# Feed-forward of a hybrid decoder step: gate and up by Strassen block products on normalised features, down projection in two parts

## The chip, the cores and the metric

One core of a Trainium2 chip runs the whole step. The metric is the device time of one execution in microseconds (us). Engines: TensorE (PE), VectorE (DVE), ScalarE (ACT), GpSimd (POOL) and SyncE (SP), whose queue issues most DMAs. Each works through its own queue in order and waits for the others on semaphores.

## The reference

Only the end of the layer is touched. With x the input, `mixed` the gated sum of the three branches:

```python
h = x + rms_norm(mixed @ w_out, norm_mix_post)
f = rms_norm(h, norm_ffn_pre)
f = (silu(f @ w_ffn_gate) * (f @ w_ffn_up)) @ w_ffn_down
y = h + rms_norm(f, norm_ffn_post)
```

There are 544 tokens (512 of the prompt, 32 of the samples), 1024 features in 8 blocks of 128, and 2816 hidden features in 22 blocks of 128. Everything is float32.

## The kernel before

Activations lie transposed, features on partitions and tokens along the columns, in two halves A and B of 272 tokens. A float32 product is made of three `float32r` matmuls: a value x is split into a high part (a cast to float32r, on ACT) and a low part (x minus the high part, on DVE), and the product is high·high + high·low + low·high. `wraw` (L197) loads a weight piece of 128x512 (256 KB) on SP's queue into a ring of five buffers, `wload` and `wk` (L202, L211) split it into `wh` and `wl`, rings of five and four. `dense` (L218) runs the three matmuls of each of k blocks into a PSUM bank per half (L228 to L230) and then calls an evacuation function. `mm_tile` hands out five PSUM banks in turn.

The stretch in question starts with the output projection (`wo`, eight blocks, first for half A, then for half B, evacuated by `normed_evac`, which also sums the squares into `ss1`). `residual(half)` (L1320) follows for each half: `col_stats` turns the sums into one factor per token (matmuls with a column of ones, L282; a root by Newton steps on DVE, L245 to L251, tiles `rs_*`; and matmuls that spread the factor over the partitions, tile `sb`, L299), `h` is scaled and `x` is added (L1328, L1329), the features are split into `fh` and `fl` without their norm (L1330, L1331), and the squares of h are summed into `ss2`. A second `col_stats` makes the factor `R2`.

Gate and up (`gate_up`, L1344): the features go into the product unnormalised, and R2 is multiplied in behind it. Gate: `m_z = p * R2`, `m_a = tanh(m_z / 2)`, `m_g = (m_a + 1) * m_z`, then once more by R2 on POOL (L1352). Up: `m_q = m_g * p`, halved and split into `dh` and `dl` (L1358, L1359). The first four blocks of hidden features (`NA`, list `first_`, weights kept split in slots by `wslots`, tiles `wsh` and `wsl`) run for half A and then for half B; the other 18 run for both halves at once. Then come the down projection over all 22 blocks, and `output`, with a third norm.

The order on each engine is set by a scheduler that walks the program with its own costs; pools and rings (their `bufs`) limit how far it can move things.

Of the kernel before, what the change touches and what calls it, by code (L numbers as in the profile page):

```python
# [157 lines left out]
def step(ctx: ExitStack, tc: tile.TileContext, I, O):  # L158
# [7 lines left out]
    NA, FB = 4, 31  # L166
# [1150 lines left out]
    fh, fl = [fslot("fh", F32R) for _ in range(8)], [fslot("fl", F32R) for _ in range(8)]  # L1317
    ss1, ss2, R2 = slot("ss1"), slot("ss2"), slot("R2")

    def residual(half):  # L1320
# [3 lines left out]
        for n in range(8):  # L1324
            x = htile("xr", 4)
# [4 lines left out]
            S.mul(fh[n][:, s:e], t, gain(G_FPRE + n))  # L1330
            V.scalar_tensor_tensor(fl[n][:, s:e], t, gain(G_FPRE + n), f32(fh[n][:, s:e]), op0=ALU.mult, op1=ALU.subtract)  # L1331
            if n == 0:
                S.square(ss2[:, s:e], t)
            else:
                q = htile("r_q", 2)
                S.square(q, t)
                G.tensor_tensor(ss2[:, s:e], ss2[:, s:e], q, op=ALU.add)
        col_stats(at, [ss2], half, D, R2, tag="at2", bufs=1)
# [4 lines left out]

    def gate_up(j, ws, half, up):  # L1344
        def gevac(p, s, e):
            z = htile("m_z", 2)
            V.tensor_tensor(z, p, R2[:, s:e], op=ALU.mult)
            t = htile("m_a")
            S.activation(t, z, AF.Tanh, scale=0.5)
            g_ = htile("m_g", 4)  # L1350
            V.scalar_tensor_tensor(g_, t, 1.0, z, op0=ALU.add, op1=ALU.mult)  # L1351
            G.tensor_tensor(g_, g_, R2[:, s:e], op=ALU.mult)  # L1352
            gz[j, s] = g_

# [73 lines left out]
```

## Time and profile before

| | |
|---|---|
| median of 3 runs | 1243.65 us (1238.79 to 1243.99) |
| the profiled execution | 1244.79 us, its span 1243.0 us |
| PE busy | 1184.3 us, 95% of the span |
| DVE, ACT, POOL busy | 664.0, 450.2, 325.2 us |
| mean granted clock of PE | 0.981 of full speed |
| chain that ended last | PE 85%, DVE 6%, DMA 4% of the span |

The span runs from the first to the last instruction. Busy times count an engine's instructions from start to end; PE's overlap in its pipeline. The feed-forward takes about the last third of the span.

### The profile page before, as it was taken

What the parts mean: (1) busy time and instruction counts of PE and PEld (TensorE: products, weight loads), DVE (VectorE), ACT (ScalarE), POOL (GpSimd) and SP (SyncE); (2) the same over time, 40 slices, a digit from 0 to 9 for tenths busy, and PEclk for the clock granted to TensorE, in tenths of its full rate; (3) what the DMA queues carried; (4) which work ended last, traced back from release to release, by engine and by line L of the source; (5) the groups of instructions that cost most, each with busy time, mean ns of one, the idle gap of its engine ahead of it and who ended that gap; (6) DMA issues with size and microseconds to landing.
All of it is one profiled execution on the core that took longest, in us unless ns stands there. A gap on an engine that the chain in (4) does not pass through costs nothing.

```text
span 1243.0 us, 24871 instructions
## 1 busy us (share of the span) xinstructions
PE 1184.3 (95%) x9495; PEld 1110.8 (89%) x9495; DVE 664.0 (53%) x1516; ACT 450.2 (36%) x1008; POOL 325.2 (26%) x344
## 2 busy tenths in 40 slices
PE   6999999999799899999899999999999999999996
PEld 6999999978687679789678999999999999999996
DVE  7697574655223223235677859387444544523346
ACT  4334434323122123134446645353333333323341
POOL 6332011211553554400344530034111112100002
PEclk9999999999899899999999999999999999999998
DMA  5332342384686777645121125122222222223343
GB/s 205 98 113 89 123 141 98 104 269 138 200 252 179 228 222 235 203 153 164 37 66 37 47 70 187 52 86 72 85 86 86 94 91 88 86 77 94 94 126 108
DMA packets 87591, 154.87 MB, mean 125 GB/s; under 512 B 11120, under 2 KB 31088, under 8 KB 87472
## 3 DMA queue, kind: packets, MB, share of 16 engines
q1 hardware_dynamic: 73072, 116.57, 29.3%
q0 software_dynamic: 6912, 23.08, 6.2%
q10 hardware_dynamic: 7488, 13.63, 3.4%
q8 instruction: 75, 1.23, 0.4%
q14 instruction: 44, 0.36, 0.1%
HBM read 145.07 MB, written 8.17 MB: 123 GB/s over the span
## 4 chain that ended last, share of the span: by engine, by line
PE 85%; DVE 6%; DMA 4%; issue 3%; ACT 1%; POOL 1%; SPq 0%; DVEq 0%; ACTq 0%; POOLq 0%
PE mm L228 23%; PE mm L229 22%; PE mm L230 22%; PE ps_sc L903 2%; PE po L958 1%; PE pvo L1239 1%; PE pv L1199 1%; PE pk L1184 1%; POOL acc L1128 1%; DMA ret_s<-s 1%; PE ps_sc L910 1%; PE ptm L1232 1%; DMA wr<-w_in 1%; DVE wl L208 1%; DVE ul L335 1%
## 5 line engine op out<-in xcount | busy, mean ns | idle before, releaser
L207 ACT CAST wh<-wr 128x512 fp32r<-128x512 f32 (+2 forms) x316 | 190.6, 605 | 365.8 <-PE mm L229 246.8
L208 DVE TENSOR_TENSOR wl<-wr,wh 128x512 fp32r<-128x512 f32 (+1 forms) x289 | 199.7, 692 | 163.0 <-PE mm L230 104.5
L228 PE MATMUL mm<-uh,wh 128*128 128x272 f32 x896 | 264.9, 297 | 7.9 <-ACT wh L207 5.6
L229 PE MATMUL mm<-ul,wh 128*128 128x272 f32 x896 | 264.1, 295 | 1.9 <-DVE ul L335 1.4
L230 PE MATMUL mm<-uh,wl 128*128 128x272 f32 x896 | 263.2, 294 | 0.4 <-DVE wl L208 0.4
L228 PEld LDWEIGHTS mm<-uh,wh 128*128 128x128 f32 x896 | 170.8, 191 | 13.9 <-ACT wh L207 5.5
L229 PEld LDWEIGHTS mm<-ul,wh 128*128 128x128 f32 x896 | 171.1, 191 | 6.1 <-issue 2.9
L229 PE MATMUL mm<-fl,wh 128*128 128x272 f32 x608 | 175.1, 288 | 0.0
L228 PE MATMUL mm<-fh,wh 128*128 128x272 f32 x608 | 175.0, 288 | 0.0
L230 PEld LDWEIGHTS mm<-uh,wl 128*128 128x128 f32 x896 | 171.3, 191 | 4.0 <-issue 2.9
L230 PE MATMUL mm<-fh,wl 128*128 128x272 f32 x608 | 174.6, 287 | 0.0
L230 PEld LDWEIGHTS mm<-fh,wl 128*128 128x128 f32 x608 | 114.6, 189 | 0.0
L228 PEld LDWEIGHTS mm<-fh,wh 128*128 128x128 f32 x608 | 114.3, 188 | 0.0
L229 PEld LDWEIGHTS mm<-fl,wh 128*128 128x128 f32 x608 | 114.3, 188 | 0.0
L228 PE MATMUL mm<-dh,wh 128*128 128x272 f32 x352 | 101.1, 288 | 0.0
L229 PE MATMUL mm<-dl,wh 128*128 128x272 f32 x352 | 101.1, 288 | 0.0
L230 PE MATMUL mm<-dh,wl 128*128 128x272 f32 x352 | 100.4, 288 | 0.0
L1352 POOL TENSOR_TENSOR m_g<-m_g,R 128x272 f32<-128x272 f32 x44 | 46.1, 1048 | 205.6 <-DVE m_g L1351 194.3
L895 POOL DMA_INDIRECT kt<-kpool,ixk x64 | 61.7, 963 | 85.4 <-DMA kt<-kpool 37.5
L228 PEld LDWEIGHTS mm<-dh,wh 128*128 128x128 f32 x352 | 66.2, 188 | 0.0
L229 PEld LDWEIGHTS mm<-dl,wh 128*128 128x128 f32 x352 | 66.1, 188 | 0.0
L230 PEld LDWEIGHTS mm<-dh,wl 128*128 128x128 f32 x352 | 65.8, 188 | 0.0
(565 smaller groups left out, 2493.8 us busy)
## 6 DMA issues: line engine op xcount, KB each, us to landing
wr<-w_in SPq DMA_DIRECT2D x80, 256.0 KB
wr<-w_fd SPq DMA_DIRECT2D x50, 256.0 KB
wr<-w_fg SPq DMA_DIRECT2D x44, 256.0 KB
wr<-w_fu SPq DMA_DIRECT2D x44, 256.0 KB
kt<-kpool SPq DMA_DIRECT2D x64, 160.0 KB
wr<-w_in ACTq DMA_DIRECT2D x32, 256.0 KB
s<-s SPq DMA_DIRECT2D x16, 256.0 KB
wr<-w_ret_o ACTq DMA_DIRECT2D x16, 256.0 KB
```

The lines of the kernel that those rows point to most:

```text
L207: S.copy(wh, raw)
L208: lo.tensor_tensor(wl, raw, f32(wh), op=ALU.subtract)
L228: PE.matmul(p[:, :e - s], lhsT=a, rhs=xh[i][:, s:e], start=i == 0, stop=False)
L229: PE.matmul(p[:, :e - s], lhsT=a, rhs=xl[i][:, s:e], start=False, stop=False)
L230: done.append(PE.matmul(p[:, :e - s], lhsT=b, rhs=xh[i][:, s:e], start=False, stop=i == nk - 1))
L335: V.scalar_tensor_tensor(l, x, gain(G_PRE + k), f32(h), op0=ALU.mult, op1=ALU.subtract)
L895: loads.append(G.indirect_dma_start(k_[:, a, :], None, kflat, bass.IndirectOffsetOnAxis(ixk[:, j:j + 1], 0)))
L903: lead = PE.matmul(o3[rows], lhsT=qlf[i][:, cols], rhs=kt[b][:, :, 128 * i:128 * i + 128].rearrange("p a (j s) -> p a j s", j=2), start=i ...
L910: PE.matmul(o3[rows, :, j, :], lhsT=qzf[j][:, cols], rhs=kt[b][:, :, 256:320], start=False, stop=i == 3)
L958: lead = PE.matmul(po[32 * b:32 * b + 32, :KVL], lhsT=pT[:, 128 * j + 32 * b:128 * j + 32 * b + 32], rhs=vt[b][:, j, :], start=False, stop ...
L1128: G.tensor_tensor(acc[n][:, s:e], acc[n][:, s:e], z, op=ALU.add)
L1352: G.tensor_tensor(g_, g_, R2[:, s:e], op=ALU.mult)
```

## The change

Eighteen of the 22 hidden blocks are taken in pairs (j, j+1). For gate, and again for up, the pair's two weight blocks form a 2x2 matrix of 128x512 pieces (a11, a12 for block j, a21, a22 for j+1, split by the two halves of the 1024 input features), and the features form a 2x2 matrix f11, f12, f21, f22 (halves of the features by halves A and B of the tokens). The eight block products are replaced by the seven of Strassen's scheme in Winograd's form. It needs four sums of feature blocks, t1 to t4, made once in `sums` and kept split, and for every pair four sums of weight pieces, made on POOL (`comb`, tiles `ws`):

s1 = a21 + a22, s2 = s1 - a11, s3 = a11 - a21, s4 = a12 - s2.

The seven products go to three PSUM banks b1, b2, b3. Bank b1 collects a11·f11, then s2·t2, then s1·t1, then s4·f22, and is copied out between them by ACT (`keep_`: p1, u2, u4); b2 collects s3·t3 (copied as p7) and a22·t4; b3 takes a12·f21. The four output blocks are b2 + u2, u4 + p7 (on POOL, tile m_y), b3 + p1, and b1 itself.

Since sums of features must be of the normalised ones, R2 and the multiplications by it go: `residual` now writes `fn`, the normalised features, after its second `col_stats`, and splits those (`form`). The first four blocks still run as plain products, half A, then `sums`, then half B. The squares of `residual` take their buffers from the same ring of three as the evacuations (`m_q`), and xT's tiles have eight buffers in place of four. The down projection runs for the first 12 blocks in the middle of the pairs (its result kept in `yb`), and for the other 10 at the end, where a sum joins the two (`y_evac`).

The core of the diff:

```diff
-    NA, FB = 4, 31
+    NA, FB = 4, 34
...
-    fh, fl = [fslot("fh", F32R) for _ in range(8)], [fslot("fl", F32R) for _ in range(8)]
-    ss1, ss2, R2 = slot("ss1"), slot("ss2"), slot("R2")
+    fn = [fslot("fn") for _ in range(8)]
+    ss1, ss2 = slot("ss1"), slot("ss2")
+    forms = {}
+    def form(name, i, x):
+        t = fslot(name, F32R)
+        hi, lo = t[:, :HALF], t[:, HALF:]
+        S.copy(hi, x)
+        V.tensor_tensor(lo, x, f32(hi), op=ALU.subtract)
+        forms[name, i] = hi, lo
     def residual(half):
         (s, e), = half
         _, (rb,) = col_stats(at, [ss1], half, D)
         for n in range(8):
-            x = htile("xr", 4)
+            x = htile("xr", 8)
             SY.dma_start(x, I["xT"][128 * n:128 * n + 128, s:e])
             t = hres[n][:, s:e]
             V.tensor_tensor(t, t, rb, op=ALU.mult)
             (G if n % 2 else V).tensor_tensor(t, t, x, op=ALU.add)
-            S.mul(fh[n][:, s:e], t, gain(G_FPRE + n))
-            V.scalar_tensor_tensor(fl[n][:, s:e], t, gain(G_FPRE + n), f32(fh[n][:, s:e]), op0=ALU.mult, op1=ALU.subtract)
             if n == 0:
                 S.square(ss2[:, s:e], t)
             else:
-                q = htile("r_q", 2)
+                q = htile("m_q")
                 S.square(q, t)
                 G.tensor_tensor(ss2[:, s:e], ss2[:, s:e], q, op=ALU.add)
-        col_stats(at, [ss2], half, D, R2, tag="at2", bufs=1)
+        _, (rb,) = col_stats(at, [ss2], half, D, tag="at2", bufs=1)
+        for n in range(8):
+            V.scalar_tensor_tensor(fn[n][:, s:e], hres[n][:, s:e], gain(G_FPRE + n), rb, op0=ALU.mult, op1=ALU.mult)
+            form(f"f{1 + n // 4}{1 if half is A else 2}", n % 4, fn[n][:, s:e])
+    def sums():
+        (a0, a1), = A
+        (b0, b1), = B
+        for i in range(4):
+            f11, f12 = fn[i][:, a0:a1], fn[i][:, b0:b1]
+            f21, f22 = fn[i + 4][:, a0:a1], fn[i + 4][:, b0:b1]
+            t1, t2, t3, t4 = [htile("xr", 8) for _ in range(4)]
+            G.tensor_tensor(t3, f22, f12, op=ALU.subtract)
+            form("t3", i, t3)
+            G.tensor_tensor(t1, f12, f11, op=ALU.subtract)
+            V.tensor_tensor(t2, f22, t1, op=ALU.subtract)
+            form("t2", i, t2)
+            V.tensor_tensor(t4, f21, t2, op=ALU.subtract)
+            form("t4", i, t4)
+            form("t1", i, t1)
     dh, dl = [], []
     gz = {}
+    def gate_out(key, z):
+        t = htile("m_a")
+        S.activation(t, z, AF.Tanh, scale=0.5)
+        g_ = gz[key] = htile("m_g", 6)
+        V.scalar_tensor_tensor(g_, t, 1.0, z, op0=ALU.add, op1=ALU.mult)
+    def up_out(key, u):
+        j, s = key
+        t = htile("m_q")
+        V.tensor_tensor(t, gz[key], u, op=ALU.mult)
+        o = slice(s, s + HALF)
+        S.mul(dh[j][:, o], t, 0.5)
+        V.scalar_tensor_tensor(dl[j][:, o], t, 0.5, f32(dh[j][:, o]), op0=ALU.mult, op1=ALU.subtract)
+    def product(p, w, x, first, last=True, skip=False):
+        wh, wl = w
+        for i in range(4):
+            a, b = wh[:, 128 * i:128 * i + 128], wl[:, 128 * i:128 * i + 128]
+            xh, xl = forms[x, i]
+            PE.matmul(p, lhsT=a, rhs=xh, start=first and i == 0, stop=False, skip_group_check=skip)
+            PE.matmul(p, lhsT=a, rhs=xl, start=False, stop=False, skip_group_check=skip)
+            PE.matmul(p, lhsT=b, rhs=xh, start=False, stop=last and i == 3, skip_group_check=skip)
     def gate_up(j, ws, half, up):
-        def gevac(p, s, e):
-            z = htile("m_z", 2)
-            V.tensor_tensor(z, p, R2[:, s:e], op=ALU.mult)
-            t = htile("m_a")
-            S.activation(t, z, AF.Tanh, scale=0.5)
-            g_ = htile("m_g", 4)
-            V.scalar_tensor_tensor(g_, t, 1.0, z, op0=ALU.add, op1=ALU.mult)
-            G.tensor_tensor(g_, g_, R2[:, s:e], op=ALU.mult)
-            gz[j, s] = g_
-        def uevac(p, s, e):
-            t = htile("m_q")
-            V.tensor_tensor(t, gz[j, s], p, op=ALU.mult)
-            S.mul(dh[j][:, s:e], t, 0.5)
-            V.scalar_tensor_tensor(dl[j][:, s:e], t, 0.5, f32(dh[j][:, s:e]), op0=ALU.mult, op1=ALU.subtract)
-        dense(ws, fh, fl, uevac if up else gevac, half)
-    def d_slots(alloc):
-        dh.append(alloc("dh", F32R))
-        dl.append(alloc("dl", F32R))
+        (s, _), = half
+        h = 1 if half is A else 2
+        p = mm_tile("mm")[:, :HALF]
+        for c, w in enumerate(ws):
+            product(p, w[:2], f"f{1 + c}{h}", c == 0, c == 1)
+        (up_out if up else gate_out)((j, s), p)
+    def pair(src, j, up):
+        out = up_out if up else gate_out
+        a11, a21, a22 = wraw(src[j][:, :512], 512), wraw(src[j + 1][:, :512], 512), wraw(src[j + 1][:, 512:], 512)
+        a12 = wraw(src[j][:, 512:], 512)
+        def hl(x):
+            wh = ring.tile([128, 512], F32R, tag="wh", name="wh", bufs=RB[1])
+            wl = ring.tile([128, 512], F32R, tag="wl", name="wl", bufs=RB[2])
+            S.copy(wh, x)
+            V.tensor_tensor(wl, x, f32(wh), op=ALU.subtract)
+            return wh, wl
+        def comb(x, y, op):
+            t = slot512("ws")
+            G.tensor_tensor(t, x, y, op=op)
+            return t
+        def keep_(p, name):
+            t = ffn.tile([128, HALF], F32, tag="xr", name=name, bufs=8)
+            S.copy(t, p)
+            return t
+        b1, b2, b3 = [mm_tile(n)[:, :HALF] for n in ("b1", "b2", "b3")]
+        product(b1, hl(a11), "f11", True, skip=True)
+        p1 = keep_(b1, "p1")
+        s3 = comb(a11, a21, ALU.subtract)
+        product(b2, hl(s3), "t3", True, skip=True)
+        p7 = keep_(b2, "p7")
+        s1 = comb(a21, a22, ALU.add)
+        s2 = comb(s1, a11, ALU.subtract)
+        product(b1, hl(s2), "t2", False, skip=True)
+        u2 = keep_(b1, "u2")
+        product(b2, hl(a22), "t4", False, skip=True)
+        z = htile("m_z", 3)
+        V.tensor_tensor(z, b2, u2, op=ALU.add)
+        out((j + 1, 0), z)
+        product(b1, hl(s1), "t1", False, skip=True)
+        u4 = keep_(b1, "u4")
+        z = htile("m_y", 2)
+        G.tensor_tensor(z, u4, p7, op=ALU.add)
+        out((j + 1, HALF), z)
+        product(b3, hl(a12), "f21", True)
+        z = htile("m_z", 3)
+        V.tensor_tensor(z, b3, p1, op=ALU.add)
+        out((j, 0), z)
+        s4 = comb(a12, s2, ALU.subtract)
+        product(b1, hl(s4), "f22", False, skip=True)
+        out((j, HALF), b1)
+    def d_slots(alloc, n=1):
+        for _ in range(n):
+            dh.append(alloc("dh", F32R))
+            dl.append(alloc("dl", F32R))
...
-        d_slots(fslot)
-    for half in (A, B):
-        for j, up, ws in first_:
-            gate_up(j, ws, half, up)
-    for j in range(NA, NF):
-        d_slots(slot if j < NA + 15 else fslot)
-        gate_up(j, wk(I["w_fg"][j]), HALVES, 0)
-        gate_up(j, wk(I["w_fu"][j]), HALVES, 1)
-    yb = [fslot("yb") for _ in range(8)]
+        d_slots(slot)
+    for j, up, ws in first_:
+        gate_up(j, ws, A, up)
+    sums()
+    for j, up, ws in first_:
+        gate_up(j, ws, B, up)
+    NB = 12
+    def pairs(j0, j1):
+        for j in range(j0, j1, 2):
+            d_slots(slot if j > j0 else fslot, 2)
+            pair(I["w_fg"], j, 0)
+            pair(I["w_fu"], j, 1)
+    pairs(NA, NB)
+    yb = [slot("yb") for _ in range(8)]
+    for n in range(8):
+        def evac(p, s, e):
+            S.copy(yb[n][:, s:e], p)
+        dense(wk(I["w_fd"][n][:, :128 * NB]), dh, dl, evac)
+    pairs(NB, NF)
+    def y_evac(n, last=None):
+        def evac(p, s, e):
+            t = yb[n][:, s:e]
+            V.tensor_tensor(t, t, p, op=ALU.add)
+            if n == 0:
+                S.square(ss3[:, s:e], t)
+            elif last is not None:
+                S.square(last[:, s:e], t)
+            else:
+                q = htile("m_q")
+                S.square(q, t)
+                V.tensor_tensor(ss3[:, s:e], ss3[:, s:e], q, op=ALU.add)
+            S.mul(t, t, gain(G_FPOST + n))
+        return evac
...
     for n in range(6):
-        dense(wk(I["w_fd"][n]), dh, dl, normed_evac(yb, ss3, n, G_FPOST))
+        dense(wk(I["w_fd"][n][:, 128 * NB:]), dh[NB:], dl[NB:], y_evac(n))
     for half in (A, B):
         for n in range(6, 8):
-            dense(wk(I["w_fd"][n]), dh, dl, normed_evac(yb, ss3, n, G_FPOST, ss4 if n == 7 and half is B else None), half)
+            dense(wk(I["w_fd"][n][:, 128 * NB:]), dh[NB:], dl[NB:], y_evac(n, ss4 if n == 7 and half is B else None), half)
```

**What moves on the queues.** First, PE where the output projection of half B ends (bank `mm_10995` before, `mm_11001` now, features `mh`, `ml`). Before:

```order
L230 MATMUL mm_10995<-mh_10132,wsl_10389 128x272
L228 MATMUL mm_10995<-mh_10238,wsh_10388 128x272
L282 MATMUL st_10768<-ones_69,ss2_10417 128x1 x3
L229 MATMUL mm_10995<-ml_10239,wsh_10388 128x272
L230 MATMUL mm_10995<-mh_10238,wsl_10389 128x272
L228 MATMUL mm_11225<-fh_10400,wsh_10651 128x272
L229 MATMUL mm_11225<-fl_10408,wsh_10651 128x272
```

Now:

```order
L229 MATMUL mm_11001<-ml_10239,wsh_10388 128x272
L230 MATMUL mm_11001<-mh_10238,wsl_10389 128x272
L282 MATMUL st_11030<-ones_69,ss1_10408 128x1 x3
L299 MATMUL sb_10764<-ident_67,rs_r_10747 128x128 x2
L299 MATMUL sb_10764<-ident_67,rs_r_10747 128x16
L299 MATMUL sb_11051<-ident_67,rs_r_11034 128x128 x2
L299 MATMUL sb_11051<-ident_67,rs_r_11034 128x16
L1392 MATMUL mm_11246<-f11_10769,wsh_10642 128x272
L1392 MATMUL mm_11275<-f11_10769,wsh_10654 128x272
```

The spreading of half A's second factor (`sb_10764`, from `rs_r_10747`) and of half B's first (`sb_11051`) now stand between the last output-projection matmul and the first of gate and up.

Second, DVE at the root of half A's second statistics. Before:

```order
L245 TENSOR_SCALAR rs_v_10773<-st_10768 128x3
L246 TENSOR_SCALAR rs_k_10776<-rs_v_10773 128x3
L247 TENSOR_SCALAR rs_y_10774<-rs_k_10776 128x3
L249 TENSOR_TENSOR rs_t_10775<-rs_y_10774 128x3
L1312 TENSOR_TENSOR ss1_10416<-ss1_10416,m_q_11020 128x272
L250 SCALAR_TENSOR_TENSOR rs_t_10775<-rs_t_10775,rs_v_10773 128x3
```

Now:

```order
L245 TENSOR_SCALAR rs_v_10748<-st_10743 128x3
L1281 TENSOR_TENSOR wsl_11175<-wr_11172,wsh_11174 128x512
L246 TENSOR_SCALAR rs_k_10751<-rs_v_10748 128x3
L1281 TENSOR_TENSOR wsl_11181<-wr_11178,wsh_11180 128x512
L247 TENSOR_SCALAR rs_y_10749<-rs_k_10751 128x3
L1281 TENSOR_TENSOR wsl_11187<-wr_11184,wsh_11186 128x512
L249 TENSOR_TENSOR rs_t_10750<-rs_y_10749 128x3
L1281 TENSOR_TENSOR wsl_11193<-wr_11190,wsh_11192 128x512
```

Low parts of gate and up weights (`wsl`, later `wl`) now lie between the steps of the root, down to its last step, which writes `rs_r_10747`.

Third, the end of a pair's up product: POOL and PE of the second pair now (12281 to 12287 are the raw pieces of up, `u4_12390` the copy of its bank `b1_12289`). Before, POOL's queue holds only `m_g` times R2 in this stretch. POOL now:

```order
L1419 TENSOR_TENSOR ws_12332<-ws_12330,wr_12281 128x512
L1444 TENSOR_TENSOR m_y_12231<-u4_12229,p7_12167 128x272
L1444 TENSOR_TENSOR m_y_12392<-u4_12390,p7_12328 128x272
L1419 TENSOR_TENSOR ws_12420<-wr_12287,ws_12332 128x512
L1419 TENSOR_TENSOR ws_12475<-wr_12446,wr_12448 128x512
```

PE now (`wh_12422` and `wl_12423` are split from `ws_12420`):

```order
L1393 MATMUL b1_12289<-t1_11555,wh_12374 128x272
L1394 MATMUL b1_12289<-t1_11555,wl_12375 128x272
L1392 MATMUL b1_12289<-f22_11151,wh_12422 128x272
L1393 MATMUL b1_12289<-f22_11151,wh_12422 128x272
L1392 MATMUL b1_12454<-f11_10769,wh_12457 128x272
L1393 MATMUL b1_12454<-f11_10769,wh_12457 128x272
L1394 MATMUL b1_12289<-f22_11151,wl_12423 128x272
```

The sum s4 (`ws_12420`) stands behind `m_y_12392`, which needs the copy of s1·t1; the two matmuls on s4's high part follow those on s1 directly.

## Rows read from the trace of the kernel before

**Rows 1.** The page: busy us and share by engine; granted clock in 40 slices, tenths
```profile
PE 1184.3 (95%) x9495; PEld 1110.8 (89%) x9495; DVE 664.0 (53%) x1516; ACT 450.2 (36%) x1008; POOL 325.2 (26%) x344
...
PEclk9999999999899899999999999999999999999998
```

**Rows 2.** Windows: busy time (x instructions) of five engines, PEclk, DMA share, GB/s
```profile
900.00:1000.00 100.00, 100.00 (x801) 100.00 (x801) 50.08 (x102) 35.27 (x68) 16.68 (x16) 1.00 0.25 88
1120.00:1220.00 100.00, 100.00 (x801) 100.00 (x800) 37.14 (x71) 36.34 (x72) 0.00 (x0) 1.00 0.37 109
```

**Rows 3.** Groups of instructions, ACT, 870 to 1220 us: busy, mean ns | idle before
```profile
L207 ACT CAST wh<-wr 128x512 fp32r<-128x512 f32 x121 | 75.2, 622 | 84.2 <-PE mm L229 81.3 <-PE mm L230 1.1 <-DVE rs_t L250 0.9
L1311 ACT ACTIVATE m_q<-mm 128x272 f32<-128x272 f32 x13 | 5.1, 394 | 8.8 <-PE mm L230 8.8
```

**Rows 4.** Timeline: start, us, engine, line, operation, count [idle before <-releaser]
```profile
800.08 2.50 DVE L1281 TENSOR_TENSOR wsl<-wr,wsh 128x512 fp32r<-128x512 f32 x4 [0.44 <-ACT wsh L1280]
809.21 2.87 DVE L1328 TENSOR_TENSOR h<-h,sb 128x272 f32<-128x272 f32 x8
799.42 2.18 ACT L1280 CAST wsh<-wr 128x512 fp32r<-128x512 f32 x4
```

**Rows 5.** Timeline of DVE and POOL where both have work
```profile
657.71 0.69 DVE L1173 TENSOR_TENSOR qs<-ra,qs 64x512 fp32r<-64x512 f32 x1
687.44 2.38 DVE L1173 TENSOR_TENSOR qs<-ra,qs 64x512 fp32r<-64x512 f32 x2 [0.39 <-ACT qs L1172]
687.70 1.58 POOL L208 TENSOR_TENSOR wl<-wr,wh 128x512 fp32r<-128x512 f32 x1 [0.95 <-PE pv L1199]
689.77 1.30 POOL L208 TENSOR_TENSOR wl<-wr,wh 128x512 fp32r<-128x512 f32 x1 [0.49 <-PE mm L230]
816.46 5.65 POOL L1337 TENSOR_TENSOR ss<-ss,r_q 128x272 f32<-128x272 f32 x6
848.05 3.78 POOL L1337 TENSOR_TENSOR ss<-ss,r_q 128x272 f32<-128x272 f32 x4
818.59 2.89 DVE L1331 SCALAR_TENSOR_TENSOR fl<-h,gains,fh 128x272 fp32r<-128x272 f32 x3
848.30 0.43 DVE L1347 TENSOR_TENSOR m_z<-mm,R 128x272 f32<-128x272 f32 x1
```

**Rows 6.** Timeline of PE and DVE about the start of gate/up, and the end
```profile
824.46 0.29 PE L230 MATMUL mm<-mh,wsl 128*128 128x272 f32 x1
824.58 0.29 PE L228 MATMUL mm<-fh,wsh 128*128 128x272 f32 x1
824.43 0.16 DVE L245 TENSOR_SCALAR rs_v<-st 128x3 f32<-128x3 f32 x1 [0.84 <-PE st L282]
824.62 0.17 DVE L246 TENSOR_SCALAR rs_k<-rs_v 128x3 int32<-128x3 int32 x1
845.26 1.26 DVE L208 TENSOR_TENSOR wl<-wr,wh 128x512 fp32r<-128x512 f32 x1
1232.37 0.16 DVE L251 SCALAR_TENSOR_TENSOR rs_r<-rs_t,rs_y 128x3 f32<-128x3 f32 x1
1233.88 0.78 DVE L1403 TENSOR_TENSOR yb<-yb,sb 128x272 f32<-128x272 f32 x2 [1.34 <-PE sb L299]
```

**Rows 7.** Timeline of one gate evacuation, 906 to 911 us
```profile
906.12 0.43 ACT L1349 ACTIVATE m_a<-m_z 128x272 f32<-128x272 f32 x1 [2.49 <-DVE m_z L1347]
906.59 0.44 DVE L1351 SCALAR_TENSOR_TENSOR m_g<-m_a,m_z 128x272 f32<-128x272 f32 x1 [0.50 <-ACT m_a L1349]
910.19 0.77 POOL L1352 TENSOR_TENSOR m_g<-m_g,R 128x272 f32<-128x272 f32 x1 [1.71 <-DVE m_g L1351]
```

**Rows 8.** Windows, 628 to 640 us, columns as in group 2
```profile
628.00:632.00 4.00, 2.48 (x11) 1.57 (x10) 3.81 (x6) 0.64 (x2) 1.54 (x2) 1.00 0.29 91
632.00:636.00 4.00, 4.00 (x20) 3.66 (x19) 2.62 (x3) 2.37 (x5) 1.86 (x2) 0.57 0.05 8
636.00:640.00 4.00, 4.00 (x30) 3.67 (x30) 2.80 (x11) 1.89 (x6) 0.54 (x1) 1.00 0.14 45
```

## The prediction

> **What bounds the kernel now.** I read the page first. TensorE (PE) is busy 95% of the span, and the clock granted to it is at 0.9 of full speed or more in 37 of 40 slices [rows 1]; the other engines are at 53% or less. So the time is the number of matmuls times their spacing. The spacing is not the duration that the page prints (0.29 us): matmuls overlap. The windows give it: 801 matmuls in 100.00 us, both in gate/up and in the down projection [rows 2], so 0.1248 us each. Removing matmuls pays 0.1248 us each, and only while the other engines keep up. What those engines need is in the groups of instructions [rows 3] and in the timeline [rows 4]: there a back-to-back run gives the slot of one instruction, which is shorter than its duration: four 512-wide low parts on VectorE (DVE) in 2.50 us, so 0.60 each; eight 272-wide operations in 2.87, so 0.35; four casts on ScalarE (ACT) in 2.18, so 0.52.
>
> **What the change removes.** Each of 9 pairs of feature blocks has, for gate and for up, 84 matmuls in place of 96. That is 9 x 2 x 12 = 216 fewer, 27.0 us at 0.1248. A pair takes 192 x 0.1248 = 23.97 us now and would take 168 x 0.1248 = 20.97 if PE never waited. The down projection keeps its 1056 matmuls.
>
> **What it adds beside PE, in a pair.** DVE: 14 low parts (8 now) and 16 operations of 272 columns (4 z, 4 m_g, 4 m_q, 4 dl): 14 x 0.60 + 16 x 0.35 = 14.0 us. ACT: 14 casts x 0.52 + 8 copies out of PSUM + 8 of 272 columns; with 0.39 for a copy (nearest row: the squares of a PSUM tile [rows 3]) and 0.43 for the others [rows 7] that is 13.8 us, under 21. GpSimd (POOL): 8 sums of 512 columns x 1.29 (a POOL low part of that size [rows 5]) and 2 of 272 x 0.77 [rows 7], 11.9 us, against 4 operations now. Weight loads stay at eight of 256 KB per pair at a DMA share of 0.25 [rows 2]: hidden, with 0.75 of the queues free.
>
> Each fits alone. DVE and POOL do not fit together. Two DVE operations (qs, 512 columns) met one POOL operation and took 2.38 us; alone one takes 0.69, and two 0.60 + 0.69 = 1.29, so the POOL operation cost DVE 1.09, and POOL itself took 1.58 instead of 1.30 [rows 5]. With 272 columns, three fl took 2.89 us beside POOL's sums, 0.96 each against 0.35, so 0.61 [rows 5]. An operation that reads PSUM (m_z at 848.30) keeps its 0.43 in the middle of POOL's work [rows 5]. In a pair, 24 of DVE's 30 operations read SBUF alone. If every POOL operation met one, DVE would need 14.0 + 8 x 1.09 + 2 x 0.61 = 23.9 us; a fifth meet a PSUM reader (10 x 0.2 x 0.35 = 0.7 off), so **23.2 us, more than PE's 20.97**. The nearest row below is no meeting at all, 14.0.
>
> [...]
>
> **A new chain in the order.** In 7 of the 9 pairs (all but the first of each stage) POOL's queue has m_y, the sum for the second half of the lower block, ahead of the last weight sum s4 of the up product. m_y needs the copy u4 of the bank that S1·T1 has just finished; and PE's next matmul is the one on s4's high part, with no other work between. So PE stands still for u4 0.39 + m_y 0.77 + s4 1.29 + cast 0.62 + four hand-overs of about 0.05 (m_a ends and m_g starts 0.04 later [rows 7]) = 3.3 us; then 0.3 more, because s4's low part (0.69) is covered by two matmuls of s4 and two of the next a11 (0.5 us). PE's path is 20.97 + 3.6 = 24.5 us. DVE waits in the same chain, so its own need overlaps it: without m_y's and s4's meetings 14.0 + 7 x 1.09 + 0.61 - 0.7 = 21.5, and 1.7 of standing still (1.2 until m_y, then 1.9 of s4 and cast less four operations of 0.35): 23.2. The two paths share the weights' order, so I add 0.5 to the longer: **25.0**. The other two pairs take 23.2. Bounds: 20.97 (all hidden, a gain) and 26.8 (DVE's 23.2 with PE's 3.6 on top). I take 25.0, nearer the upper end, because the chain is fixed in three queues. Sum: 7 x 25.0 + 2 x 23.2 = 221.4 against 9 x 23.97 = 215.7: **+5.7 us where 27.0 were removed**.
>
> **The start of gate/up.** Before, the raw features go in unnormalised, and PE passes from the last output-projection matmul (824.46) to the first fh matmul (824.58) without a gap [rows 6]; R2 is applied behind the product. Now no feature exists until the second statistics of half A have come back through DVE, and the order gives PE nothing else. On DVE, 11 weight low parts (7 wsl, 4 wl), one sum and 22 tiny root steps stand between rs_v and the first fn: 11 x 0.60 + 0.35 + 22 x 0.20 (rs_v to rs_k [rows 6]) = 11.4 us. The statistics cannot start before POOL's squares are summed, at 822.1 before [rows 5]; I take 822, so fn at 833.4; with 0.35, a cast of 0.43 and hand-overs the first matmul is at 834.3, **+9.7 us**. Bounds: +2 if only the 11 root steps of half A count (2.2) with the 1.35 from rs_r to the first use of sb [rows 6]; +24 if the low parts run as late as before (the last ended at 846.5 [rows 6]). I take 9.7, what the queue holds. The split of half A (8 fn, 16 casts and low parts), half B, and 16 sums with their forms run beside 48 us of half products; half B's statistics are summed while PE does half A, and DVE needs for sums and forms 36 operations x 0.35 + 8 x 0.61 = 17.5 of 24 us: no cost while that cover lasts. If it went, the first pair would start late by what is left of the 17.5.
>
> **Small terms.** The squares of residual A and of the output projection now share three m_q buffers, so evacuating block 1 waits for POOL: 0.8 (0 to 3). xT's eight buffers stop the loads on SP's queue from standing behind residual B, a gain off the path: 0. The extra evacuation of the down projection (16 copies) lies beside 72 us of matmuls: 0. The last tile has a DVE sum ahead of its square: 0.44, 0.5 with its hand-over. Entering and leaving two pair stages: 1.1 (0 to 4).
>
> **Sum.** 5.7 + 9.7 + 0.8 + 0.5 + 1.1 = +17.8. The profiled execution took 1244.8 (span 1243.0 and 1.8 around it), so 1262.6; the median shown, 1243.65, is 1.1 lower, so **1261 us**, 1.4% slower. About 0.5% (6 us) can be told from no change here.
>
> **Rivals.**
> - *PE stays the bound (faster).* The meetings fall into DVE's free time and s4 is done early. Pairs take 21.0: -27.0 + 12.1 = -14.9, **1229**. For it: PE's order has 22 matmuls (2.7 us) of other products between most copies and the next use of their bank. Against it: 14.0 + 8.2 of DVE already exceed 21. It decides below 22.6 per pair, where 9 x (23.97 - 22.6) pays the 12.1.
> - *Gain and loss cancel.* Pairs at 22.6, **1244**. It needs the start at 9.7 and half the chain hidden.
> - *The clock falls.* In 628 to 632 us PE was busy 2.48 of 4.00 us, and in the next 4 us the granted clock was 0.57, near the lower level, then 1.00 [rows 8]. If each of the 7 stops does that for 4 us, 4 x 0.43 = 1.7 us each: +12, **1273**. Against it: at 628 PE had been idle more often before.
> [...]
>
> **How the numbers follow.** Forecast 0.42, PE-bound 0.17, cancel 0.17, clock 0.14, lock 0.10. Slower by over 0.5%: 0.42 + 0.14 + 0.10, less 0.02 of the forecast's lower tail, 0.64; faster 0.17; within, the 0.19 left. The forecast's own range is 1248 to 1272. The range takes in "cancel" and its start at +4 (1238) and, above, pairs of 26.8 with the start at 9.7 (1280); only the fast case and a late start lie outside.
>
> **What would show it.** Right: 216 fewer matmuls at unchanged spacing; a PE gap of 8 to 12 us ahead of the first f11 matmul that ends on DVE or ACT; in the pair stages about 168 matmuls in 23 to 25 us, PE waits on ACT's casts of ws behind POOL's m_y, and DVE low parts above 0.69 on average. Wrong: 168 matmuls in 21 us, or no gap at the start.

## The result and the profile after

| | before | after |
|---|---|---|
| median of 4 runs each, same chip | 1242.16 us | 1299.78 us |
| profiled execution (span) | 1244.79 (1243.0) | 1299.73 (1297.9) |
| mean granted clock | 0.981 | 0.953 |
| matmuls recorded | 9495 | 9279 (216 fewer) |

The ratio is 1.0462 [1.0433, 1.0490]: slower, as forecast, but by 57.6 us and not 17.8. 1261 us was forecast, with a range up to 1280: the time lies outside.

The page of the changed kernel, the lines that answer to [rows 1], and a group that is new:
```profile
PE 1182.1 (91%) x9279; PEld 1106.3 (85%) x9279; DVE 762.3 (59%) x1610; ACT 508.3 (39%) x1160; POOL 404.4 (31%) x398
...
PEclk9999999998899899999999999899888999888897
...
L1419 POOL TENSOR_TENSOR ws<-wr 128x512 f32<-128x512 f32 x36 | 54.7, 1527 | 105.5 <-DMA wr<-w_fg 68.0
```
PE's busy time is that of before, with 216 fewer matmuls: "busy" hides most of the loss, since a matmul at a lower clock counts as busy for longer (below, 19 fill the 4.00 us from 968 to 972 at 0.50, and 560 the 70.00 from 1010 to 1080 at 1.00). The granted clock has new slices at 8 late in the span. Windows of all five engines (columns as in [rows 2]) over two stretches of regular pairs, the first of them one pair from start to start; then over the first pair of each stage; then over the first part of the down projection:
```profile
937.70:969.60 31.90, 23.88 (x170) 23.11 (x170) 23.83 (x31) 13.85 (x30) 13.12 (x10) 0.87 0.19 66
1104.00:1136.00 32.00, 24.56 (x172) 23.83 (x171) 23.02 (x30) 13.84 (x30) 13.17 (x11) 0.84 0.19 67
884.70:906.30 21.60, 21.45 (x170) 21.02 (x169) 18.06 (x25) 13.08 (x28) 13.17 (x9) 1.00 0.29 101
1071.40:1092.50 21.10, 21.10 (x170) 20.97 (x169) 14.93 (x24) 12.95 (x28) 10.28 (x7) 1.00 0.28 100
1010.00:1080.00 70.00, 70.00 (x560) 70.00 (x559) 18.65 (x28) 22.07 (x44) 12.20 (x9) 1.00 0.29 89
```
A regular pair takes **31.9 us** (written as 32.0 in the texts below); 25.0 was forecast. The first pair of each stage, which has no stop, takes 21.6 and 21.1; 23.2 was forecast. The waits of PE over both pair stages (total, times, longest) say where PE stands:
```profile
PE b L1392 <- ACT wh L1413: 34.4, 7, 5.2
PE b L1394 <- DVE wl L1414: 12.3, 8, 2.2
PE b L1392 <- DVE m_q L1381: 0.8, 2, 0.5
```
Seven stops, the number forecast, at the place forecast; but on average 4.9 us each for the high part of s4 (3.3 forecast) and 1.8 more for a low part (0.3). One of them in the timeline, engine by engine, from S1·T1's last matmul on:
```profile
958.51 0.29 PE L1394 MATMUL b<-t,wl 128*128 128x272 f32 x1
964.01 0.60 PE L1392 MATMUL b<-f,wh 128*128 128x272 f32 x1 [5.21 <-ACT wh L1413]
967.58 0.59 PE L1394 MATMUL b<-f,wl 128*128 128x272 f32 x1 [2.23 <-DVE wl L1414]
...
958.83 0.39 ACT L1424 COPY u<-b 128x272 f32<-128x272 f32 x1 [1.29 <-PE b L1394]
961.60 0.43 ACT L1383 ACTIVATE dh<-m_q 128x272 fp32r<-128x272 f32 x1 [2.38 <-DVE m_q L1381]
963.02 0.43 ACT L1383 ACTIVATE dh<-m_q 128x272 fp32r<-128x272 f32 x1 [0.99 <-DVE m_q L1381]
963.35 0.60 ACT L1413 CAST wh<-ws 128x512 fp32r<-128x512 f32 x1
...
960.08 1.48 DVE L1381 TENSOR_TENSOR m_q<-m_g,m_y 128x272 f32<-128x272 f32 x1 [1.96 <-POOL m_y L1444]
961.49 1.50 DVE L1381 TENSOR_TENSOR m_q<-m_g,m_z 128x272 f32<-128x272 f32 x1
962.91 2.94 DVE L1384 SCALAR_TENSOR_TENSOR dl<-m_q,dh 128x272 fp32r<-128x272 f32 x2
965.77 1.75 DVE L1414 TENSOR_TENSOR wl<-ws,wh 128x512 fp32r<-128x512 f32 x1
...
959.29 0.75 POOL L1444 TENSOR_TENSOR m_y<-u,p 128x272 f32<-128x272 f32 x1 [9.05 <-ACT u L1424]
960.00 1.26 POOL L1419 TENSOR_TENSOR ws<-wr,ws 128x512 f32<-128x512 f32 x1
961.22 2.89 POOL L1419 TENSOR_TENSOR ws<-wr 128x512 f32<-128x512 f32 x2
```
Read it from below. POOL stood behind m_y for 9.05 us, waiting for u4, and then ran m_y, s4 and the next block's sums in one burst. s4 was done at 961.26, as forecast. But its cast came at 963.35: ACT's queue has two dh ahead of it, and these wait for two m_q that the burst stretched from 0.44 us to 1.5 each. Two dl (2.94) then stand ahead of s4's low part (1.75, alone 0.69). The stop feeds itself: the wait bunches POOL's sums, and the bunch slows the DVE instructions for which ACT waits.

The clock after the stop (PE alone: busy, count, PEclk, DMA share, GB/s):
```profile
956.00:960.00 4.00, 2.79 (x23) 1.00 0.00 0
960.00:964.00 4.00, 0.00 (x0) 0.88 0.18 66
964.00:968.00 4.00, 1.77 (x6) 0.50 0.18 66
968.00:972.00 4.00, 4.00 (x19) 0.50 0.18 68
972.00:976.00 4.00, 4.00 (x30) 0.84 0.44 132
```
PE was idle from about 958.8 to 964.0; from 964 the granted clock was 0.50 until past 972. While PE was busy for the whole of 968 to 972, only 19 matmuls ran in those 4 us. So 31.9 = 20.97 of matmuls + 7.4 of stops + 3.5 of half clock and tails.

The whole stage (with the down projection's first part in it, 576 matmuls, 71.9 us) is the measure for the experiments. It is taken between the two starts in this row of the matmul groups, from the first pair matmul to some 0.5 us before the last:
```profile
L1392 PE MATMUL b<-f,wh x216: 282/288/596, 884.7 to 1216.5; 128*128 128x272 f32 x108
```
That is 331.8 us. Matmuls alone need 188.7 + 71.9 = 260.6; I had forecast 221.4 + 71.9 = 293.3. **The 38.5 us between forecast and stage make up the miss: 1261 + 38.5 = 1299.5.** That the sum comes out to the microsecond is luck, as single runs differ by more. The stops take 47.5 of the 71.2 above the matmuls; summed over windows of 2 us, busy time x (1 - PEclk), the clock takes 19.6; some 4 are left, which I put down, as an estimate, to matmuls that end alone (0.29 us at 958.51, 0.60 at 964.01, against a spacing of 0.1248). Against the forecast this is 22.3 more for the stops (47.5 in place of 7 x 3.6), 19.6 for the clock, 4.1 of rest, and 7.5 less for what DVE was to cost beside the chain (0.43 in each of seven pairs, 2.2 in each of two).

At the start of gate/up the DVE order came as forecast: the last output-projection matmul at 822.0, the first f11 matmul at 832.47:
```profile
821.99 0.28 PE L230 MATMUL mm<-mh,wsl 128*128 128x272 f32 x1
...
829.07 1.43 PE L299 MATMUL sb<-ident,rs_r 128*128 128x128 f32 x6 [4.66 <-DVE rs_t L250]
...
832.47 1.25 PE L1392 MATMUL mm<-f,wsh 128*128 128x272 f32 x4
```
A gap of 10.4 us, 9.7 forecast. Behind it the clock was low as well, which no term of the forecast held:
```profile
832.00:838.00 6.00, 6.00 (x33) 0.61 0.00 2
```
By the sum of busy time x (1 - PEclk) that is 2.2 us more.

### The profile page after: what moved, and what is told of

Same layout as the page of the kernel before. It is cut to its first block, busy times and chain, and to the rows that moved or that the text cites. A ratio compares the mean times of both kernels' runs of the same rounds, so it can differ in the third digit from the quotient of the medians.

```text
span 1297.9 us, 24803 instructions
## 1 busy us (share of the span) xinstructions
PE 1182.1 (91%) x9279; PEld 1106.3 (85%) x9279; DVE 762.3 (59%) x1610; ACT 508.3 (39%) x1160; POOL 404.4 (31%) x398
## 4 chain that ended last, share of the span: by engine, by line
PE 74%; DVE 10%; issue 7%; POOL 3%; DMA 3%; ACT 2%; another core or an unknown queue 0%; SPq 0%; DVEq 0%; POOLq 0%; ACTq 0%
PE mm L228 16%; PE mm L230 15%; PE mm L229 15%; PE b L1394 3%; PE b L1392 3%; PE b L1393 3%; DVE wl L1414 2%; PE po L958 2%; DVE m_q L1381 1%; PE ps_sc L903 1%; PE pvo L1239 1%; DVE dl L1384 1%; PE mm L1393 1%; PE mm L1392 1%; PE mm L1394 1%
## 5 line engine op out<-in xcount | busy, mean ns | idle before, releaser
L207 ACT CAST wh<-wr 128x512 fp32r<-128x512 f32 (+2 forms) x238 | 141.4, 599 | 268.5 <-PE mm L229 160.0
L208 DVE TENSOR_TENSOR wl<-wr,wh 128x512 fp32r<-128x512 f32 (+2 forms) x211 | 146.5, 697 | 137.6 <-PE mm L230 83.6
L1392 PE MATMUL b<-f,wh 128*128 128x272 f32 x216 | 70.0, 324 | 35.1 <-ACT wh L1413 34.4
L1419 POOL TENSOR_TENSOR ws<-wr 128x512 f32<-128x512 f32 x36 | 54.7, 1527 | 105.5 <-DMA wr<-w_fg 68.0
L1392 PE MATMUL b<-t,wh 128*128 128x272 f32 x288 | 83.9, 291 | 0.0
L1393 PE MATMUL b<-t,wh 128*128 128x272 f32 x288 | 83.7, 291 | 0.0
L1394 PE MATMUL b<-t,wl 128*128 128x272 f32 x288 | 82.6, 287 | 0.0
L1394 PE MATMUL b<-f,wl 128*128 128x272 f32 x216 | 69.5, 322 | 12.5 <-DVE wl L1414 12.3
L1392 PEld LDWEIGHTS b<-f,wh 128*128 128x128 f32 x216 | 46.4, 215 | 37.2 <-ACT wh L1413 35.9
L1393 PE MATMUL b<-f,wh 128*128 128x272 f32 x216 | 68.1, 315 | 0.0
```

The source lines that it names most:

```text
L207: S.copy(wh, raw)
L208: lo.tensor_tensor(wl, raw, f32(wh), op=ALU.subtract)
L1392: PE.matmul(p, lhsT=a, rhs=xh, start=first and i == 0, stop=False, skip_group_check=skip)
L1393: PE.matmul(p, lhsT=a, rhs=xl, start=False, stop=False, skip_group_check=skip)
L1394: PE.matmul(p, lhsT=b, rhs=xh, start=False, stop=last and i == 3, skip_group_check=skip)
L1419: G.tensor_tensor(t, x, y, op=op)
```

## Experiments

The time of one execution carries several microseconds from the stages ahead (with the same code there, the output projection's last matmul came between 819.7 and 829.2, and at 791.8 on the chip of no_sums) and from the chip. So the table gives the kernel before on the same chip, and the stage as measured above: its length, PE's idle time in it, and the clock's share. The stage repeats far better: where two runs differ only ahead of it, its length agreed within 0.8 us (root_first with the change; start_on_pool and ahead_root_first, 292.4, with ahead_my_dve; both_more, 286.5, with deeper_ahead).

| run | us | before | stage | idle | clock |
|---|---|---|---|---|---|
| the change | 1299.8 | 1242.2 | 331.8 | 47.7 | 19.6 |
| my_on_dve | 1280.5 | 1247.5 | 308.6 | 28.9 | 12.7 |
| s4_early | 1285.2 | 1247.5 | 316.5 | 36.1 | 13.6 |
| filler | 1313.6 | 1247.5 | 338.6 | 20.8 | 9.9 |
| ahead | 1283.9 | 1242.2 | 312.2 | 27.3 | 14.0 |
| ahead_my_dve | 1257.1 | 1242.2 | 291.6 | 19.0 | 1.6 |
| deeper_ahead | 1258.2 | 1242.6 | 287.1 | 14.6 | 3.4 |
| root_first | 1305.1 | 1242.2 | 331.4 | 47.6 | 18.9 |
| start_on_pool | 1271.3 | 1242.6 | 291.5 | 19.5 | 0 |
| no_sums | 1197.1 | 1216.3 | 264.1 | 0 | 0 |

plain_blocks, ahead_root_first and both_more were executed three or four times, the change four times, the others once.

**plain_blocks: the change without its pairs.**
```diff
-            pair(I["w_fg"], j, 0)
-            pair(I["w_fu"], j, 1)
+            for i in (j, j + 1):
+                for up in range(2):
+                    ws = wk(I["w_fu" if up else "w_fg"][i])
+                    for half in (A, B):
+                        gate_up(i, ws, half, up)
```


> Edit: normalised features and the down projection in two parts stay; the 18 blocks from the fifth on are plain again (gate_up for both halves, as for the first four), so no block products of Strassen's, and no sums of features. Theory: the start of gate/up costs 9.7 us and the two-part down projection 1 to 2, the rest of the loss is in the pairs: 1244.8 + 11 = 1256 us (1252 to 1262). Rival (the pairs cost it all, the rest nothing): 1243 to 1247 us. Rival (half of the loss lies outside the pairs): 1270 us.

Measured: 1259.5 against 1247.5, 1.0087 [1.0057, 1.0117]: +12.1 us (7 to 15). My terms that this kernel still holds were 9.7 + 0.8 + 0.5 = 11.0 (the 1.1 was for entering and leaving pair stages). So the miss is not there, and about 45 of the change's 57.6 us are the pairs'. The single terms are not shown by this: the gap at the start was 11.0 us here, and the low clock behind it is in the 12.1 too.

**my_on_dve: m_y off POOL.**
```diff
-        G.tensor_tensor(z, u4, p7, op=ALU.add)
+        V.tensor_tensor(z, u4, p7, op=ALU.add)
```


> Edit: the sum m_y (u4 + p7) goes from GpSimd to VectorE; nothing else. Changed kernel: 1299.7 us in its profiled run, seven stops of TensorE that sum to 34.4 us (waiting for the cast of s4's weights on ScalarE) plus 12.3 us (waiting for their low part on VectorE), regular pair 32.0 us. Theory (the chain u4 copy, m_y, s4 behind it on GpSimd, and the half clock that follows a stop): GpSimd no longer stands behind u4, its sums are done early, and what is left of a stop is u4 0.39 + m_y 0.43 + m_q 0.43 + two dh 0.8 + cast 0.62 = 2.7, with about 1 for the low part: 3.7 instead of 6.7, so 21 us less, and up to 16 us more where the clock stays up: 1263 to 1279 us, pair 25 to 28. Rival (VectorE and GpSimd in each other's way set the pair, whatever the order): VectorE gets more to do, pair 31 to 32.5, 1295 us or more.

Measured: the stage is 23 us shorter, though DVE does more: the rival of the two engines alone falls. The time, 1280.5 on a chip where the kernel before took 1247.5, is within the theory's range if 5 us are allowed for the chip; its regular pairs, 27.2 to 29.9 us, lie at the top of the 25 to 28 or above. What is left of a stop is the rest of the chain, in the timeline of one of them (ACT, DVE, ACT, PE):
```profile
1137.66 0.39 ACT L1424 COPY u<-b 128x272 f32<-128x272 f32 x1 [1.29 <-PE b L1394]
...
1138.08 0.85 DVE L1444 TENSOR_TENSOR m_y<-u,p 128x272 f32<-128x272 f32 x1 [1.12 <-ACT u L1424]
1138.96 0.44 DVE L1381 TENSOR_TENSOR m_q<-m_g,m_y 128x272 f32<-128x272 f32 x1
...
1139.44 0.78 ACT L1383 ACTIVATE dh<-m_q 128x272 fp32r<-128x272 f32 x2 [1.39 <-DVE m_q L1381]
1140.13 0.60 ACT L1413 CAST wh<-ws 128x512 fp32r<-128x512 f32 x1
...
1140.78 0.58 PE L1392 MATMUL b<-f,wh 128*128 128x272 f32 x1 [3.16 <-ACT wh L1413]
```
The cast of s4 no longer waits for s4, only for its place behind two dh, and m_q is back at 0.44: with no burst of sums beside it, it is not stretched.

**s4_early: the other end of the same queue.**
```diff
         s2 = comb(s1, a11, ALU.subtract)
+        s4 = comb(a12, s2, ALU.subtract)
...
-        s4 = comb(a12, s2, ALU.subtract)
         product(b1, hl(s4), "f22", False, skip=True)
```


> Edit: the sum s4 = a12 - s2 is written right behind s2, so that it stands ahead of m_y in GpSimd's queue; m_y stays on GpSimd. Theory of the chain: s4 and its cast come in time, and the stop moves behind the f22 product, to the t3 product of the next pair, whose cast stands on ScalarE behind four dh: m_q 0.43 + dh 0.40 + cast 0.62 and about 1 for the low part, 2.5 instead of 6.7: 29 us less, and up to 16 us for the clock: 1255 to 1271 us. If m_y on GpSimd does the harm wherever it stands (it still waits there for u4, with the sums of the next pair behind it), the stop is as long as before at another product: 1290 us or more. Rival of the engines in each other's way: the same work on the same engines, 1295 us or more.

Measured: the stage is 15 us shorter, less than the theory wanted. The stop did move to the next pair's t3 product, but there it still lasted up to 4.3 us: POOL still waited 9.31 us behind m_y, and its burst still stretched m_q and dl (1.50 each). So s4's place is not the whole of it; the same wait of POOL in front of a bunch of sums made a stop at another product.

**ahead and ahead_my_dve: the block's end in another order.**
```diff
+        s4 = comb(a12, s2, ALU.subtract)
...
+        product(b3, hl(a12), "f21", True)
+        product(b1, hl(s4), "f22", False, skip=True)
+        after = prep(*nxt) if nxt else None
         z = htile("m_y", 2)
-        G.tensor_tensor(z, u4, p7, op=ALU.add)
+        V.tensor_tensor(z, u4, p7, op=ALU.add)
         out((j + 1, HALF), z)
-        product(b3, hl(a12), "f21", True)
...
-        s4 = comb(a12, s2, ALU.subtract)
-        product(b1, hl(s4), "f22", False, skip=True)
```
prep() loads the next block, splits a11, and sums and splits s3. The line with V is in ahead_my_dve alone; ahead keeps G.

> Edit: the program of a block is written in another order, with the same instructions on the same engines: the loads, the sum s3 and the casts for the next block's f11 and t3, and s4 with its cast, are written ahead of m_y, of the sum on p1 and of the dh and dl that follow from them. m_y stays on GpSimd. In the queues m_y now stands behind s4 and the next block's s3, and s4's cast and the next block's two casts stand ahead of the three dh that follow from u4. Theory (the order at the block's end makes the stops): what is left of a stop is u4 0.39 + cast 0.62 + 0.1, and some 0.4 for the low part, 1.5 in each of seven pairs, 10 us in all instead of 46.7 (m_y on ACT my_on_dve had left 27.3), and the clock stays up, another 5 to 16 us: 1248 to 1264 us against 1299.7 (some 5 us more on the chip of the last four runs, where the kernel before took 1247.5 and not 1242.2). Rival (m_y on GpSimd is the harm wherever it stands, since the sums s1 and s2 of the next block are still behind it): the stop moves to the t2 product, 1270 to 1290 us. Rival (GpSimd's and VectorE's collisions alone): 1295 us or more.

> Edit: as in the run ahead, and m_y on VectorE as in my_on_dve. Theory: the stop at f22 as there, 1.5 us a pair, and nothing behind it, since no sum waits for u4 and VectorE's m_y is short (0.43, or 0.85 where GpSimd is at work): 1245 to 1260 us (5 more on the slower chip), pair 22.5 to 24. Rival (VectorE's own work is now the bound, 23.2 us a pair by the rows before and 0.9 more for the two m_y): pair 24 to 25, 1258 to 1270 us.

(In the first text, "had left 27.3" is meant of my_on_dve, m_y on VectorE.) Measured: order alone leaves 27.3 us of idle time (a rival's case, 1270 to 1290: the stop went to the t2 product). Order and m_y on DVE leave 19.0 in stops of at most 1.3 us, and the clock is all but whole again. PE's waits, of ahead and then of ahead_my_dve:
```profile
PE b L1392 <- ACT wh L1407: 23.1, 12, 3.2
PE b L1394 <- DVE wl L1408: 4.0, 11, 0.6
```
```profile
PE b L1394 <- DVE wl L1408: 8.7, 9, 1.3
PE b L1392 <- ACT wh L1407: 7.0, 7, 1.0
PE b L1392 <- ACT p L1418: 1.6, 4, 0.6
```
Between these two only m_y's engine differs: 20.6 us of stage. ahead_my_dve's pairs take (291.6 - 71.9) / 9 = 24.4 us, still no gain on 23.97. That this is near the forecast's mean of 24.6 is luck: the first pair of each stage takes 21.5 and 21.0 and the regular ones, from start to start, 24.1 to 26.7. The time lies in the theory's range and the pair in the rival's; what sets it is left open here.

**filler: what the clock costs.**
```diff
-        product(b1, hl(s1), "t1", False, skip=True)
+        w1 = hl(s1)
+        product(b1, w1, "t1", False, skip=True)
+        for _ in range(3 * up):
+            product(b2, w1, "t1", True, skip=True)
```


> Edit: in the up block of each pair 36 matmuls more, behind the S1 T1 product, into a bank that nobody reads (the product once more, three times): 36 x 0.125 = 4.5 us of TensorE work in each of nine pairs, 40 us in all, right where TensorE stood still for 4.9 us in seven of them. Theory with the clock as a price of its own (the stop costs its length and then some 2 to 3.6 us at half clock): the clock stays at 1.00, the stops are filled, the two pairs without a stop get 4.5 us longer: 1300 + 9 - 16 = 1293 us, pair 28 to 29.5 and not 32. Rival (the pair is set by the other engines alone and the clock costs nothing): pair 32, 1309 us. Rival (the added matmuls delay the chain itself): up to 1340 us.

Measured: 40.4 us of matmuls more, and the stage is only 6.8 longer. A regular pair, and the wait that is left in it:
```profile
949.30:982.00 32.70, 28.85 (x206) 27.98 (x206) 24.05 (x31) 13.63 (x30) 13.24 (x10) 0.92 0.20 65
...
979.99 0.60 PE L1394 MATMUL b<-f,wl 128*128 128x272 f32 x1 [2.52 <-DVE wl L1414]
```
Idle time fell by 26.9 and the clock's share by 9.7. But the pair takes 32.7 us, not 28 to 29.5, and the total is the first rival's 1309 with 5 us for the chip: my theory missed. The stops for low parts stayed (16.9 us in all), and the clock still fell behind them. So PE had room in the stops for most of the added work; that the clock has a price of its own, beside the length of the chain, this run does not show.

**no_sums: what POOL costs in the pairs.**
```diff
-        t = slot512("ws")
-        G.tensor_tensor(t, x, y, op=op)
-        return t
+        return x
```


> Edit: ahead_my_dve (1257.1 us, pair stage of 219.7 us where its matmuls alone need 188.7) without GpSimd's 72 sums of weight blocks: where a sum was taken, its first operand is taken as it is, so the output is not the reference's. Casts, low parts, products and sums on VectorE and ScalarE stay. Theory (what is left of the loss in the pairs is GpSimd at work beside VectorE: each sum of 1.3 to 1.6 us lengthens a VectorE instruction by about 1.1 us, eight a pair, and s4 comes late): the pair stage falls to 192 to 202 us, 1229 to 1240 us in all, below the kernel before (1242), so that this sum is what keeps the change from paying. Rival (the chain at the block's end and VectorE's own 15 to 16 us a pair make the rest, not GpSimd): the pair stage stays above 212 us, 1250 us or more.

Measured: 264.1 us of stage (192.2 without the down projection's part, as the theory had it), and PE without a gap. A window in the pairs, all five engines (columns as in [rows 2]):
```profile
914.00:938.00 24.00, 24.00 (x194) 24.00 (x193) 18.77 (x38) 15.36 (x34) 0.00 (x0) 1.00 0.37 107
```
Without the sums the products alone bring 1197.1 against 1216.3 for the kernel before on that chip, one execution of each. The run takes away both the collisions and the sums' lateness, and does not tell them apart.

**root_first and start_on_pool: the start of gate/up.**
```diff
-            lo.tensor_tensor(wl, raw, f32(wh), op=ALU.subtract)
+            later(lo.tensor_tensor(wl, raw, f32(wh), op=ALU.subtract))
```
```diff
-            first_.append((j, up, wslots(src, slot) if j < NA - 1 else wk(src)))
+            first_.append((j, up, wslots(src, slot, G) if j < NA - 1 else wk(src, G)))
```
The first is root_first, where later() adds a dependence on the last root step of half A; the second is start_on_pool, which starts from ahead_my_dve.

> Edit: the changed kernel, with one thing else: the 16 low parts on VectorE of the weights of the second to fourth gate and up blocks are made to wait for the last instruction of the A half's root, so that the root's twelve small instructions stand together in VectorE's queue and not one by one between low parts of 0.69 us (819.43 to 828.77 us in the changed kernel, 9.3 us). Theory: the root takes 12 x 0.2 = 2.4 us, the first gate/up matmul starts 5 to 6 us earlier, some of it is given back as the low parts come later: 3 to 6 us less, 1294 to 1297 us against 1299.7 (5 more on the slower chip), and the two waits for the column sums (5.5 and 5.4 us) fall below 2 and 3. Rival (the start is set by the sum of squares or by the loads, the low parts only fill a gap): within 2 us of the changed kernel.

> Edit: ahead_my_dve (1257.1 us), with one thing else: the low parts of the weights of the second to fourth gate and up blocks are formed on GpSimd, which stands idle there, and not on VectorE. Theory (the start of gate/up costs what VectorE has to do ahead of it; root_first only moved the stop from the A half to the B half, since VectorE's work stayed the same): VectorE has 16 x 0.69 = 11 us less between the end of the out-projection and the B half, the A root takes some 3 us instead of 9.3, and no stop comes at the B half: 4 to 8 us less, 1249 to 1253 us (5 more where the kernel before takes 1247). Rival (GpSimd's low parts, some 1.3 us each, hold up VectorE's small instructions of the root as its sums hold up VectorE in the pairs, 16 x 1.1 us at most): 1257 to 1268 us.

Measured: 1305.1 and 1271.3, both worse than the theories and worse than their rivals. The times also hold what came ahead; from the output projection's last matmul to the first pair matmul it is 66.5 us against the change's 62.7, and 68.8 against 63.7 in ahead_my_dve, so 4 to 5 us of loss. In root_first A's root took 2.3 us, and PE's gap there all but went; then half B lost more than that. PE in three windows:
```profile
828.00:850.00 22.00, 22.00 (x165) 0.92 0.39 123
850.00:860.00 10.00, 5.21 (x39) 0.94 0.00 0
860.00:870.00 10.00, 7.40 (x36) 0.54 0.01 2
```
The low parts now stood between the steps of B's root (827.00 to 839.50). The gap moved with DVE's work. In start_on_pool, POOL's six low parts in a row met the root (DVE, then POOL):
```profile
826.42 0.15 DVE L245 TENSOR_SCALAR rs_v<-st 128x3 f32<-128x3 f32 x1
826.61 1.31 DVE L246 TENSOR_SCALAR rs_k<-rs_v 128x3 int32<-128x3 int32 x1
827.95 1.22 DVE L247 TENSOR_SCALAR rs_y<-rs_k 128x3 int32<-128x3 int32 x1
829.20 1.18 DVE L249 TENSOR_TENSOR rs_t<-rs_y 128x3 f32<-128x3 f32 x1
...
838.32 0.49 DVE L1347 SCALAR_TENSOR_TENSOR fn<-h,gains,sb 128x272 f32<-128x272 f32 x1
...
826.59 7.43 POOL L1281 TENSOR_TENSOR wsl<-wr,wsh 128x512 fp32r<-128x512 f32 x6 [3.38 <-PE mm L229]
838.18 1.37 POOL L1281 TENSOR_TENSOR wsl<-wr,wsh 128x512 fp32r<-128x512 f32 x1 [4.16 <-ACT wsh L1280]
```
Six root steps of 0.16 us, one after the other, each took as long as one POOL instruction; the step before them, which reads PSUM, kept its 0.15.

**deeper_ahead, both_more, ahead_root_first.** The first adds to ahead_my_dve the next block's s1, s2 and t2 cast ahead of the block's end, and the casts for t1, f21 and f22 ahead of t1's product; both_more puts start_on_pool's edit on top of that, and ahead_root_first root_first's on ahead_my_dve.

> Edit: ahead_my_dve (1257.1 us), with the next block's s1, s2 and the cast for t2 written ahead of the block's end too, and the casts for t1, f21 and f22 ahead of t1's product. Theory: of the two stops that a pair has left (about 1 us at f22 and 1 to 2 us at the next block's t3 and t2, 18 us in all), the second goes where t2's cast no longer stands behind dh: 5 to 9 us less, 1248 to 1252 us. Rival (the queue of VectorE is the bound at the block's end: 4 low parts, m_q and dl there in 7 us, some of them behind a sum on GpSimd at 1.6 to 1.8 us instead of 0.69): within 3 us of 1257.

> Edit: start_on_pool and deeper_ahead together. Theory: both gains add, 1241 to 1248 us where the kernel before takes 1242: level with it. Rival: 1253 us or more, and the change stays slower than the kernel before however the queues are ordered, as VectorE and GpSimd hold each other up.

> Edit: ahead_my_dve and root_first together. Theory: the two add up: 3 to 6 us below ahead_my_dve, 1240 to 1257 us on the faster chip, so level with the kernel before or 1 per cent slower. Rival: what the start gains is lost at the first pair, whose weights are then late: the time of ahead_my_dve.

Measured: deeper_ahead's stage is 4.5 us shorter, its total the same, as its rival had it; both_more 1.0169 [1.0137, 1.0202] and ahead_root_first 1.0176 [1.0144, 1.0207] against the kernel before. No version that computes the reference beats it.

## Why the prediction was wrong in size

- *Matmuls removed, 27.0 us:* right, 216 fewer at the same spacing. no_sums shows the gain when nothing stands in its way.
- *Start of gate/up, +9.7, and small terms, +2.4:* the gap was right, 10.4, and so was its place on DVE. The low clock behind it, 2.2, was put at nothing. plain_blocks, +12.1 where 11.0 of these terms are left in it, bears out their sum; the small ones were not measured one by one.
- *DVE needs 23.2 us a pair beside POOL:* as a sum it is near, DVE being busy for 23.0 to 23.8 us of a regular pair. As a bound it is not borne out: the two pairs without the chain took 21.6 and 21.1 where it gave 23.2, with DVE busy for 18.06 and 14.93 us and PE nearly without a wait. In ahead_my_dve, with the order mended, pairs take 24.4 on average and DVE is busy for 61.15 of 72 us. Collisions of the size I took are there; that they set the 24.4 was not shown.
- *The new chain, 3.6 us in 7 of 9 pairs:* **this step failed, in its size.** Place, number and mechanism were right. I added up the chain of data (u4, m_y, s4, cast) and left out what stands in ACT's and DVE's queues ahead of its last links: two dh ahead of the cast, two dl ahead of the low part, all slowed by the burst of sums that the wait itself had bunched. 6.7 us per stop in place of 3.6, 22.3 of the 38.5 us.
- *The clock, a rival at 0.14:* **this step failed too: the forecast's sum had nothing for it.** It fell in all seven stops, on top of the chain, and took 19.6 us, not the rival's 12 (by the sum of busy time x (1 - PEclk); no run takes the clock away alone). It was no alternative but a consequence: seven stops of 3.3 us were already in my forecast, and [rows 8] had shown what follows one of them (its 0.57 is 0.50 from 633 to 635 in windows of 1 us). ahead_my_dve's stops of up to 1.3 us cost 1.6 of clock. In windows of 1 us the trace of the change shows 0.50 behind each of the seven stops, for 6 to 9 us from the matmul that ended it.
- *PE stays the bound, or gain and loss cancel:* both fell. *"Lock", 0.10 in the chances:* that each POOL operation costs DVE its full length is shown by no run; the nine m_q that follow m_y take 1.48 to 1.52 against 0.44, 1.05 more than alone beside sums of 1.26, near the 1.09 I took. As the bound of the pair in the change it falls too, since order alone moved the stage by 20 us.

## What to carry to other kernels

A stop is priced by the queues, not by the data: at each link of the chain, list what stands ahead of it on that engine and what that waits for. Where a step makes PE stand still again and again, the stop and the clock behind it belong in one sum (here 47.5 and 19.6 us). GpSimd, held by an early wait of 9.05 us, did its backlog in a burst, and VectorE paid for it in the very chain that PE waited for (m_q at 1.5 us in place of 0.44): put waiting sums on the engine that has nothing queued behind them.

## What was not expected of the hardware

In start_on_pool, GpSimd's low parts held up even tiny VectorE instructions: steps on 128 x 3 elements went from 0.16 us to between 1.18 and 1.31, one step per GpSimd instruction of about 1.24, while fn, which reads one operand from PSUM, kept 0.49 beside one of 1.37. The number of inputs made no such difference: rs_t, a product of two inputs, took 1.18, and rs_k, with a single input of 12 bytes per partition, 1.31. Why so small an instruction takes so long, no run here shows.
